# Chunk products with the two heads in turn, and the first block's mixer in another order

## The chip, the core and the metric

The kernel runs on one core of a Trainium2 chip. The metric is the device time of one execution in microseconds (us), the median of three runs. A core has TensorE (PE, with its weight loads listed apart as PEld), VectorE (DVE), ScalarE (ACT), GpSimd (POOL) and SyncE (SP), each with an instruction queue of its own that runs in order. Three of them issue DMAs here: SP, ACT and POOL.

## The reference, cut to what matters

Two transformer blocks of depth 2 each run one after the other on 512 tokens with 1024 channels. The change touches the attention and convolution part ("mixer") of the first block and the gated delta net of the second.

```python
# first block, per layer, between two feed-forward nets
q, k, v, ca, cg = jnp.split(u @ w_in[i], SPLITS, axis=-1)      # 512, 128, 128, 512, 512 columns
q = _partial_rope(q.reshape(B, S, 8, 64), positions)           # 8 heads of 64
k = _partial_rope(k.reshape(B, S, 2, 64), positions)           # 2 key heads
attn = _sliding_window_attention(q, k, v, sinks[i])            # blocks of 128, window 128, softmax with a sink
conv = _conformer_conv(ca, cg, conv_w[i], ...)                 # ca*sigmoid(cg), 31 taps per channel, layer norm, silu
mixed = jnp.concatenate([_rms_norm(attn, ...), _rms_norm(conv, ...)], axis=-1)
h = h + mixed @ w_out[i]

# second block, per layer: gated delta rule in chunks of 64 tokens, 6 heads of 64
lower = jnp.where(strict, einsum('bhncd,bhnsd->bhncs', k_beta, k) * decay, 0.0)   # per head, chunk: 64x64
sol = triangular_solve(lower, concatenate([v * beta, k_beta * exp(g)]), lower=True, unit_diagonal=True)
attn = einsum('bhncd,bhnsd->bhncs', q, k) * decay
# then a scan over the 8 chunks with a 64x64 state per head
```

## The kernel before, in words

Activations stand transposed: 128 channels on the partitions, 512 tokens along the free dimension. A product with a large weight is done in three matmuls of 512 columns per 128x128 weight tile (`mm3`, lines 258 to 262: high by high, high by low, low by high). The weights come as raw chunks of four tiles (256 KB) through SP's queue, four ahead (`_fetch`); ACT makes the high part (line 233) and VectorE the low part (line 234). Their order in DRAM is the order of use and is fixed on the host (`perm` and `lead`, lines 1734 to 1769).

The order on each engine is made by the framework when the kernel is built: of the instructions whose inputs are ready by its own reckoning, the one that stands earliest in the program goes first. So a unit of filler work that stands in the program between two dependent steps covers the wait between them. Such fillers are Python generators in `self.side`; `fill` takes a number of units from one, and `pace` (line 740) does so at a rate beside a chosen instruction, at most four such instructions ahead (`LAG`).

First block, `mixer1` (line 453). Line 455 starts four columns at once (gate and value of convolution channels 0 and 1); the loop of line 470 computes the eight `ca`/`cg` columns, gates them (lines 473 to 476) and sends each result to DRAM and back (lines 479 and 483, SP's queue), which spreads 32 channels over four shifted copies, `u4` (two buffers). Then come k, v (lines 488 and 489) and four q columns (line 509) with their rotation (`rope`) on VectorE. The convolution `conv(j)` (line 516) builds diagonal weights (line 519) and runs 8 groups of 4 matmuls with 32 output columns each, two instructions per matmul; a group is one filler unit. Attention is `scores(n)`, `values(n)` and `outs(n)` for four blocks of 128 tokens: two score matmuls per head (lines 548 and 549), eviction with mask and minimum (line 552), Exp (line 560), transposes (line 582), copy (line 584) and value products (line 586, through `mm2`, line 267). Convolution groups are paced beside them, 0.6 units per pair of heads in `scores` and 0.8 in `values`, one before the first score, and what is left after the last block (line 621). A layer norm over the four convolution results follows (lines 622 to 641); the products `pA` with the attention half of `w_out` run beside it and those with the other half, `pB`, after it.

Second block, class `Gdn`. Two heads share a tile, one on partitions 0 to 63 and one on 64 to 127. A product per chunk and head is a 64x64 matmul from a head's half of one tile and of another into its half of one PSUM bank; `chunks8` (line 1374) issues all 16 of them. It is called by `swap` (line 1466, a transpose), in `pre` (line 1549), by `mms` (line 1556, six times in each `inverse`) and at the end of `inverse` (line 1634). The scan (line 1648 and on) and `quarters` (line 1616) issue the two heads in turn. Fillers beside all this are the columns of the second block's input product.

PSUM has eight banks. Around the first block they are two `ps`, two `pa`, two `po`, one `px` and one `pc` (line 1689).

Of the kernel before, what the change touches and what calls it, by code (L numbers as in the profile page):

```python
# [13 lines left out]
AF = mybir.ActivationFunctionType  # L14
OP = mybir.AluOpType
# [3 lines left out]
T = 512  # L19
# [20 lines left out]
NSA_SCAN = 1.5  # L40
ORDER = ((0, 0), (1, 0), (0, 1), (1, 1), (2, 0), (2, 1), (3, 0), (3, 1))
DL_ACT = 3
FILL_FIRST = 1
AT_NORM = (4, 5, 4, 3, 3)
SQ_MIX = 1
PE_AT = 4
# [5 lines left out]
SUB_RATE = 0.35  # L52
ROWS = 1
SQ_DVE = 7
FILL_ATT = (.6, .8)
UBUFS = 2
LAG = 4
NEG = -1e30
# [59 lines left out]
class Net:  # L118
# [333 lines left out]

    def mixer1(self, i):
        nc = self.nc
        xs, rs = self.lead("pag", 4, gain=self.vec(f"mix{i}", 0, 8), at=AT_NORM[1])
        con = self.tp.tile([128, 4], F32, name="con", tag="con")
        nc.vector.tensor_scalar(con, self.vec(f"con{i}", 0, 4), 0.5, None, OP.mult)
        nsink = self.tp.tile([128, 8], F32, name="nsink", tag="nsink")
# [8 lines left out]
            nc.vector.tensor_tensor(diag, diag, self.ident[:, a:a + 32], OP.add)  # L467
        self.band = self.tp.tile([128, 256], F32, name="band", tag="band")
        nc.scalar.dma_start(self.band, self.A["band"])
        for j in range(4):  # L470
            pa, pg = self.lin("pag", xs), self.lin("pag", xs)
            a, g = self.t(name="ca", tag="c"), self.t(name="cg", tag="c")
            nc.vector.tensor_tensor(g, pg, rs, OP.mult)
            nc.scalar.activation(g, g, AF.Tanh, scale=0.5)
            nc.vector.tensor_tensor(a, pa, rs, OP.mult)
            nc.vector.scalar_tensor_tensor(a, g, 1.0, a, OP.add, OP.mult)

            um = self.tc.dram_tile([128, T], F32, name="um")
            nc.sync.dma_start(um, a)
            x = self.tp.tile([128, 4, T], F32, name="u4", tag="u4", bufs=UBUFS)  # L480
            nc.gpsimd.memset(x[:, :, 0:3], 0.0)
            for t in range(4):
                nc.sync.dma_start(x[t * 32:t * 32 + 32, :, t:], um.rearrange("(g f) x -> f g x", g=4)[:, :, :T - t])
            U4.append(x)
        cosr, sinr = self.t(name="cosr", tag="q"), self.t(name="sinr", tag="q")
        nc.vector.tensor_tensor(cosr, self.trig[0], rs, OP.mult)
        nc.vector.tensor_tensor(sinr, self.trig[1], rs, OP.mult)
        kr = self.rope(self.lin("pk", xs), cosr, sinr, 8, "qt")
        pv = self.lin("pv", xs)
        vT = self.t(name="vT")  # L490
        nc.vector.tensor_tensor(vT, pv, rs, OP.mult)
        pt = self.pat("vt")
# [13 lines left out]
            ks.append(y)  # L506
            kl.append(low)
        for j in range(4):
            x = self.rope(self.lin("pq", xs), cosr, sinr, 8, "qt")
            for g in range(2):  # L510
                y = self.t(F32R, "qs", "q")
                nc.scalar.copy(y[H[g]], x[H[g]])
                nc.vector.tensor_tensor(y[H[1 - g]], x[H[g]], y[H[g]].bitcast(F32), OP.subtract)
                qs.append(y)

        def conv(j):

            w = self.tp.tile([128, 32, 32], F32, name="cd", tag="cd", bufs=2)
            nc.vector.tensor_tensor(w, diag.unsqueeze(1).to_broadcast([128, 32, 32]),
                                    cs[:, j * 32:j * 32 + 32].unsqueeze(2).to_broadcast([128, 32, 32]), OP.mult)  # L520
            us4, pc = U4[j], self.bank("pc", "pc")
            for q in range(8):
                for g in range(4):
                    nc.tensor.matmul(pc[g * 32:g * 32 + 32, 4 * q:], w[:, g * 8 + q], us4[:, g, :T - 4 * q],
                                     start=q == 0, stop=q == 7, skip_group_check=True)
                yield
            y = self.t(name="y", tag="cp")
            nc.scalar.activation(y, pc, AF.Identity, bias=self.vec(f"cb{i}", j))
            ys.append(y)

        self.side, self.paced = dict(conv=chain(*(conv(j) for j in range(4)))), []
        mixA = [(self.x("mH"), self.x("mL")) for _ in range(4)]
        sink = self.vec(f"sink{i}", 0, 8)
        st = {}
# [1 line left out]
        def scores(n):  # L536
            k0 = max(n - 1, 0)
            w = (n - k0 + 1) * 128
            S = [self.t(name="S", tag="S") for _ in range(4)]
            nm = self.s(8, name="nm")  # L540
            for g in range(2):
                for j in range(4):
                    if j % 2 == 0:
                        ps = self.bank("scores", "sc")
                    hd = g * 4 + j
                    f = slice(j % 2 * 256, j % 2 * 256 + w)
                    q, b, k = qs[2 * j + g], slice(n * 128, (n + 1) * 128), slice(k0 * 128, (n + 1) * 128)
                    nc.tensor.matmul(ps[:, f], q[:, b], ks[g][:, k], start=True, stop=False)
                    last = nc.tensor.matmul(ps[:, f], q[:, b], kl[g][:, k], start=False, stop=True)
                    if j % 2:  # L550
                        self.pace(last, conv=FILL_ATT[0])
                    nc.vector.tensor_tensor_reduce(S[j][:, g * 256:g * 256 + w], ps[:, f],
                                                   self.band[:, 256 - w:], -0.125, nsink[:, hd:hd + 1],
                                                   OP.add, OP.min, nm[:, hd:hd + 1])
            den = self.s(8, name="den")
            for j in range(4):
                for g in range(2):
                    hd = g * 4 + j
                    x = S[j][:, g * 256:g * 256 + w]
                    nc.scalar.activation(x, x, AF.Exp, scale=-1.0, bias=nm[:, hd:hd + 1], accum_out=den[:, hd:hd + 1])  # L560
            es = self.s(8, name="es")
            nc.vector.tensor_tensor(es, sink, nm, OP.add)
            nc.scalar.activation(es, es, AF.Exp)
            nc.vector.tensor_tensor(den, den, es, OP.add)
            rd = self.s(8, name="rd")
            nc.vector.reciprocal(rd, den)
            st[n] = (S, rd)

        def values(n):
            S, rd = st[n]  # L570
            k0 = max(n - 1, 0)
            nk = n - k0 + 1
            w = nk * 128
            po = self.out_ps()
            for hd in range(8):
                j, g = hd % 4, hd // 4
                if hd % 2 == 0:
                    pp = self.pat("pp")
                    pT = self.t(name="pT", tag="p")
                b = (hd % 2) * 256  # L580
                for kb in range(nk):
                    nc.tensor.transpose(pp[:, b + kb * 128:b + kb * 128 + 128],
                                        S[j][:, g * 256 + kb * 128:g * 256 + kb * 128 + 128], self.ident)
                nc.scalar.copy(pT[:, b:b + w], pp[:, b:b + w])
                for kb in range(nk):
                    last = self.mm2(po[:, hd * 64:hd * 64 + 64], pT[:, b + kb * 128:b + kb * 128 + 128],
                                    v[:, (k0 + kb) * 128 + g * 64:(k0 + kb) * 128 + g * 64 + 64],
                                    start=kb == 0, stop=kb == nk - 1)
                if hd % 2:
                    self.pace(last, conv=FILL_ATT[1])  # L590
            st[n] = (po, rd)

        def outs(n):
# [15 lines left out]
            for j in range(4):  # L609
                self.split_to(mixA[j][0][:, c], mixA[j][1][:, c], pt[:, j * 128:(j + 1) * 128], self.vec(f"aon{i}", j))  # L610

        self.fill("conv", FILL_FIRST)
        scores(0)
        for n in range(4):
            if n < 3:
                scores(n + 1)
            values(n)
            if n:
                outs(n - 1)
        outs(3)  # L620
        self.fill("conv", None)
        a, b = self.t(name="ya", tag="c"), self.t(name="yb", tag="c")
        nc.vector.tensor_tensor(a, ys[0], ys[1], OP.add)
        nc.vector.tensor_tensor(b, ys[2], ys[3], OP.add)
# [27 lines left out]
    def ple(self, pT, gain, norm, last=False):  # L652
# [9 lines left out]

        def proj():
            for m in range(8):
                pe = self.out_ps("pe")
                self.linear(pe, ps_)
                e = self.t(name="e", tag="a")
                nc.scalar.copy(e, pe)
                es.append(e)
            r.append(self.rstd_end(self.squares(es, SQ_PE), D))  # L670
# [702 lines left out]

def chunks8(f):

    for _, s in H2:
        for c in range(8):
            f(s, slice(c * 64, c * 64 + 64))


# [291 lines left out]
def build(tc, A, plan, out):  # L1672
    with ExitStack() as ctx:
# [5 lines left out]
        with n.phase(n=2, na=1, r=3), n.psum(ps=2, pa=2, pat=("pa",)):  # L1679
# [3 lines left out]
            for big, steps in groupby(enumerate(plan), lambda x: x[1][:-1] == "mix2_"):  # L1683
                if big:
# [1 line left out]
                        with n.phase(cd=4, gq=5, gs=6, gp=12, gat=3, v=4), tc.tile_pool(name="sp2", bufs=1) as n.sp2:  # L1686
                            n.mixer2(int(step[-1]), at and plan[at - 1] == "fin1_0")
                    continue
                with n.psum(po=2, px=1, pc=1, lin=("ps", "po", "ps", "po", "px"), scores=("ps", "px", "ps"),
                            gate=("ps", "px", "ps", "pc", "po", "po")):  # L1690
                    for at, step in steps:
                        k, i = step[:-1], int(step[-1])
                        after = plan[at + 1] if at + 1 < len(plan) else ""
# [56 lines left out]
def host(I):  # L1750
# [13 lines left out]
    for nm in ("ffn1", "ffn2"):  # L1764
        A[nm] = np.stack([ffn(I[nm + "_w_gate_up"][i], I[nm + "_w_down"][i]) for i in range(2)])
    q = np.concatenate([np.r_[j * 64:j * 64 + 64, (4 + j) * 64:(4 + j) * 64 + 64] for j in range(4)])
    perm = np.concatenate([np.r_[768 + j * 128:896 + j * 128, 1280 + j * 128:1408 + j * 128] for j in range(4)]
                          + [np.r_[512:768], q])
    A["w_in"] = each(I["w_in"], lambda w: pack(w[:, perm], lead([(m, k) for m in range(14) for k in range(8)], 4)))
    A["w_out"] = each(I["w_out"], lambda w: pack(w, [(m, k) for q in ((0, 1, 2, 3), (4, 5, 6, 7)) for m in range(8) for k in q]))  # L1770

# [150 lines left out]
```

## Time and profile before

| | us |
|---|---|
| median of 3 runs | 3725.37 (3722.95 to 3727.85) |
| the profiled execution | 3727.08 |
| its span, first to last instruction | 3725.3 |
| busy in the span: TensorE | 3654.2 |
| VectorE | 2307.7 |
| ScalarE | 1563.1 |
| GpSimd | 155.9 |

The profile is of one execution. Busy time of an engine is the time in which at least one of its instructions is listed as running; the matmuls overlap in their pipeline and their ends are modelled, so a busy TensorE can still be one that runs below its rate. To see that, one looks at when matmuls start. The time of a group of equal matmuls runs from the first one's start to the last one's end. The granted clock is TensorE's clock as a share of 2.4 GHz; the two levels are 1.2 and 2.4 GHz.

### The profile page before, as it was taken

Reading aid. Unit: us, or ns where it says so; the run is one execution under the profiler, and the core shown is the slowest. Engines: PE = TensorE matmul, PEld = TensorE weight load, DVE = VectorE, ACT = ScalarE, POOL = GpSimd, SP = SyncE. Lnnn points to the kernel's source line nnn. Section 1 sums busy time; section 2 is a strip of 40 time slices with the busy share of each in tenths; the row PEclk is TensorE's granted clock in tenths of the full one; section 3 lists DMA queues with packets and bytes.
Section 4 is the critical chain, followed back from the end, with each engine's and each line's share of the span. In section 5 each row is a group of like instructions: output and inputs, shape, how many; then the busy total and the mean of one; then the engine's idle time right before and its main releaser. Section 6 shows DMA issues by size and latency. Waiting matters only on the chain. (4 is left out here: it accounts for less than half of the span.)

```text
span 3725.3 us, 55291 instructions
## 1 busy us (share of the span) xinstructions
PE 3654.2 (98%) x20946; PEld 2902.1 (78%) x20946; DVE 2307.7 (62%) x4820; ACT 1563.1 (42%) x2974; POOL 155.9 (4%) x164
## 2 busy tenths in 40 slices
PE   9999999999999999999999999999999999999998
PEld 7888757888888886688887777778887777778887
DVE  5444666444653456753448777775667786786667
ACT  4233354333532334532335344553445344653345
POOL 0000000000100000100001000000001000000001
PEclk9999999999999999999999999999999999999999
DMA  4333413333333333233333212133334112133332
GB/s 130 97 97 98 118 43 88 98 98 97 99 97 97 98 108 91 56 99 96 97 104 95 66 41 78 48 99 97 97 97 134 49 44 62 54 94 99 97 97 90
DMA packets 178955, 329.84 MB, mean 89 GB/s; under 512 B 20096, under 2 KB 24576, under 8 KB 178688
## 3 DMA queue, kind: packets, MB, share of 16 engines
q1 hardware_dynamic: 171648, 312.00, 29.8%
q10 hardware_dynamic: 5760, 10.12, 0.8%
q0 software_dynamic: 1280, 4.20, 0.3%
q8 instruction: 164, 2.69, 0.3%
q14 instruction: 103, 0.84, 0.1%
HBM read 317.84 MB, written 8.39 MB: 88 GB/s over the span
## 5 line engine op out<-in xcount | busy, mean ns | idle before, releaser
L233 ACT CAST wH<-raw 128x512 fp32r<-128x512 f32 x1116 | 691.7, 621 | 1433.5 <-PE pgu L261 457.6
L234 DVE TENSOR_TENSOR wL<-raw,wH 128x512 fp32r<-128x512 f32 x1116 | 790.7, 709 | 594.6 <-ACT wH L233 564.8
L260 PE MATMUL pgu<-xH,wH 128*128 128x512 f32 x1408 | 549.0, 390 | 9.8 <-ACT wH L233 5.9
L261 PE MATMUL pgu<-xL,wH 128*128 128x512 f32 x1408 | 550.8, 391 | 6.1 <-DVE xL L314 6.1
L262 PE MATMUL pgu<-xH,wL 128*128 128x512 f32 x1408 | 550.4, 391 | 0.8 <-DVE wL L234 0.6
L260 PE MATMUL pd<-H,wH 128*128 128x512 f32 x1056 | 410.8, 389 | 0.0
L261 PE MATMUL pd<-L,wH 128*128 128x512 f32 x1056 | 410.8, 389 | 0.0
L262 PE MATMUL pd<-H,wL 128*128 128x512 f32 x1056 | 410.8, 389 | 0.0
L260 PEld LDWEIGHTS pgu<-xH,wH 128*128 128x128 f32 x1408 | 265.1, 188 | 65.5 <-ACT wH L233 5.9
L261 PEld LDWEIGHTS pgu<-xL,wH 128*128 128x128 f32 x1408 | 265.9, 189 | 61.8 <-DVE xL L314 6.7
L262 PEld LDWEIGHTS pgu<-xH,wL 128*128 128x128 f32 x1408 | 265.9, 189 | 56.9 <-DVE wL L234 1.8
L260 PE MATMUL pup<-xH,wH 128*128 128x512 f32 x704 | 274.8, 390 | 2.1 <-DVE h L899 1.2
L262 PE MATMUL pup<-xH,wL 128*128 128x512 f32 x704 | 274.0, 389 | 0.0
L261 PE MATMUL pup<-xL,wH 128*128 128x512 f32 x704 | 273.9, 389 | 0.0
L260 PEld LDWEIGHTS pd<-H,wH 128*128 128x128 f32 x1056 | 198.2, 188 | 41.3
L261 PEld LDWEIGHTS pd<-L,wH 128*128 128x128 f32 x1056 | 198.2, 188 | 41.1
L262 PEld LDWEIGHTS pd<-H,wL 128*128 128x128 f32 x1056 | 198.2, 188 | 41.0
L349 POOL TENSOR_TENSOR ssum<-ssum,sq 128x512 f32<-128x512 f32 x72 | 110.7, 1537 | 2546.2 <-ACT sq L348 2544.9
L260 PEld LDWEIGHTS pup<-xH,wH 128*128 128x128 f32 x704 | 132.1, 188 | 31.3 <-DVE h L899 2.0
L261 PEld LDWEIGHTS pup<-xL,wH 128*128 128x128 f32 x704 | 132.2, 188 | 27.4
L262 PEld LDWEIGHTS pup<-xH,wL 128*128 128x128 f32 x704 | 132.2, 188 | 27.3
L1350 DVE SCALAR_TENSOR_TENSOR y<-x,vecs,y 128x511 f32<-128x511 f32 (+1 forms) x176 | 131.2, 749 | 17.4 <-ACT y L1347 14.7
(571 smaller groups left out, 6063.1 us busy)
## 6 DMA issues: line engine op xcount, KB each, us to landing
raw<-ffn SPq DMA_DIRECT2D x791, 256.0 KB, 2.6
raw<-w_in SPq DMA_DIRECT2D x164, 256.0 KB, 2.6
raw<-w_out SPq DMA_DIRECT2D x80, 256.0 KB, 2.7
raw<-w_ple_gate SPq DMA_DIRECT2D x80, 256.0 KB, 2.7
away<-h ACTq DMA_DIRECT2D x16, 256.0 KB, 2.1
raw<-cmp SPq DMA_DIRECT2D x16, 256.0 KB, 2.7
h<-away POOLq DMA_DIRECT2D x16, 256.0 KB, 4.2
h<-xT SPq DMA_DIRECT2D x8, 256.0 KB, 5.3
```

The lines of the kernel that those rows point to most:

```text
L233: nc.scalar.copy(H, r)
L234: nc.vector.tensor_tensor(L, r, H.bitcast(F32), OP.subtract)
L260: nc.tensor.matmul(ps, w[0], x[0], start=first, stop=False)
L261: nc.tensor.matmul(ps, w[0], x[1], start=False, stop=False)
L262: nc.tensor.matmul(ps, w[1], x[0], start=False, stop=last)
L349: (nc.vector if k >= adds else nc.gpsimd).tensor_tensor(acc, acc, q, OP.add)
L1350: nc.vector.scalar_tensor_tensor(y[:, s:], x[:, :T - s], w[:, f * 3 + tap:f * 3 + tap + 1], y[:, s:], OP.mult, OP.add)
```

## The change

`chunks8` goes over the chunks and, in each, over the two heads. In `mixer1` k, v and the q columns come first (four of these six in the leading group). The `ca`/`cg` columns become a generator `gated(j)` with one unit per triple of matmuls, gate column first; its DRAM round trip goes through POOL's queue. A convolution is one unit in place of eight. Columns and convolutions form one chain of fillers, 16 units of it ahead of the first scores, then 1.8 per pair of heads in `scores` and 2 in `values`; what is left comes before the last `outs`. The banks are dealt anew: scores rotate over the two `ps`, attention values use one `po`, the new columns use `px` and a new `py`. On the host the columns of `w_in` are permuted to match.

```diff
-FILL_FIRST = 1
+FILL_FIRST = 16
-FILL_ATT = (.6, .8)
+FILL_ATT = (1.8, 2)
@@ mixer1
-        xs, rs = self.lead("pag", 4, gain=self.vec(f"mix{i}", 0, 8), at=AT_NORM[1])
+        xs, rs = self.lead("pkvq", 4, gain=self.vec(f"mix{i}", 0, 8), at=AT_NORM[1])
...
-        for j in range(4):
-            pa, pg = self.lin("pag", xs), self.lin("pag", xs)
-            a, g = self.t(name="ca", tag="c"), self.t(name="cg", tag="c")
-            nc.vector.tensor_tensor(g, pg, rs, OP.mult)
-            nc.scalar.activation(g, g, AF.Tanh, scale=0.5)
-            nc.vector.tensor_tensor(a, pa, rs, OP.mult)
+
+        def gated(j):
+
+            g, a = self.t(name="cg", tag="c"), self.t(name="ca", tag="c")
+            for x, name in ((g, "pg"), (a, "pa")):
+                p = self.bank("cols", name)
+                yield from self.linear_g(p, xs)
+                nc.vector.tensor_tensor(x, p, rs, OP.mult)
+                if x is g:
+                    nc.scalar.activation(g, g, AF.Tanh, scale=0.5)
             nc.vector.scalar_tensor_tensor(a, g, 1.0, a, OP.add, OP.mult)
 
             um = self.tc.dram_tile([128, T], F32, name="um")
-            nc.sync.dma_start(um, a)
+            nc.gpsimd.dma_start(um, a)
             x = self.tp.tile([128, 4, T], F32, name="u4", tag="u4", bufs=UBUFS)
             nc.gpsimd.memset(x[:, :, 0:3], 0.0)
             for t in range(4):
-                nc.sync.dma_start(x[t * 32:t * 32 + 32, :, t:], um.rearrange("(g f) x -> f g x", g=4)[:, :, :T - t])
+                nc.gpsimd.dma_start(x[t * 32:t * 32 + 32, :, t:], um.rearrange("(g f) x -> f g x", g=4)[:, :, :T - t])
             U4.append(x)
...
@@ conv(j)
                 for g in range(4):
                     nc.tensor.matmul(pc[g * 32:g * 32 + 32, 4 * q:], w[:, g * 8 + q], us4[:, g, :T - 4 * q],
                                      start=q == 0, stop=q == 7, skip_group_check=True)
-                yield
             y = self.t(name="y", tag="cp")
             nc.scalar.activation(y, pc, AF.Identity, bias=self.vec(f"cb{i}", j))
             ys.append(y)
-
-        self.side, self.paced = dict(conv=chain(*(conv(j) for j in range(4)))), []
+            yield
+
+        self.side, self.paced = dict(fill=chain(gated(0), gated(1), conv(0), gated(2), conv(1), gated(3), conv(2), conv(3))), []
...
@@ end of attention
-        self.fill("conv", FILL_FIRST)
+        self.fill("fill", FILL_FIRST)
         scores(0)
...
+        self.fill("fill", None)
         outs(3)
-        self.fill("conv", None)
@@ ple
-                pe = self.out_ps("pe")
+                pe = self.bank("pe", "pe")
@@ chunks8
-    for _, s in H2:
-        for c in range(8):
+    for c in range(8):
+        for _, s in H2:
             f(s, slice(c * 64, c * 64 + 64))
@@ build
-                with n.psum(po=2, px=1, pc=1, lin=("ps", "po", "ps", "po", "px"), scores=("ps", "px", "ps"),
-                            gate=("ps", "px", "ps", "pc", "po", "po")):
+                with n.psum(po=1, px=1, py=1, pc=1, lin=("ps", "po", "ps", "py", "px"), scores=("ps",), cols=("px", "py"),
+                            gate=("ps", "px", "ps", "pc", "po", "py"), pe=("po", "py")):
@@ host
-    perm = np.concatenate([np.r_[768 + j * 128:896 + j * 128, 1280 + j * 128:1408 + j * 128] for j in range(4)]
-                          + [np.r_[512:768], q])
+    perm = np.concatenate([np.r_[512:768], q] + [np.r_[1280 + j * 128:1408 + j * 128, 768 + j * 128:896 + j * 128] for j in range(4)])
```

## Rows read from the trace of the kernel before

**Rows 1.** The page, section 1: busy us, share of the span, instructions

```profile
PE 3654.2 (98%) x20946; PEld 2902.1 (78%) x20946; DVE 2307.7 (62%) x4820; ACT 1563.1 (42%) x2974; POOL 155.9 (4%) x164
```

**Rows 2.** Timeline of PE, one chunk product: start, length, line, count

```profile
2065.58 1.90 PE L1549 MATMUL pkk<-kb,y 64*64 64x64 f32 x32
2067.40 0.50 PE L261 MATMUL pqkv<-xL,wH 128*128 128x512 f32 x1
```

**Rows 3.** Timeline of PE, two chunk products back to back and their seam

```profile
2118.27 1.72 PE L1556 MATMUL py<-X,TT 64*64 64x64 f32 x29
...
2119.94 0.22 PE L1556 MATMUL pyt<-TT,X 64*64 64x64 f32 x1
2119.95 0.22 PE L1556 MATMUL py<-X,TT 64*64 64x64 f32 x1
2120.00 1.67 PE L1556 MATMUL pyt<-TT,X 64*64 64x64 f32 x29
2121.60 0.50 PE L260 MATMUL psq<-xH,wH 128*128 128x512 f32 x1
```

**Rows 4.** Timeline of PE, a step of the scan

```profile
2143.61 0.33 PE L1648 MATMUL pvd<-S,kbg 64*64 64x64 f32 x4
```

**Rows 5.** Windows: length, busy of PE, PEld, DVE, ACT, POOL; granted clock; DMA

```profile
452.60:459.00 6.40, 3.17 (x19) 2.42 (x17) 6.22 (x21) 5.51 (x16) 0.00 (x0) 0.94 0.23 59
459.00:470.00 11.00, 10.99 (x56) 4.14 (x55) 4.49 (x22) 4.72 (x22) 0.00 (x0) 0.72 0.04 14
...
452.60:528.50 75.90, 72.64 (x594) 32.06 (x592) 38.92 (x158) 38.37 (x129) 0.23 (x2) 0.96 0.16 36
...
1444.00:1463.00 19.00, 17.01 (x82) 8.15 (x84) 10.12 (x39) 10.05 (x35) 0.00 (x0) 0.73 0.11 28
```

**Rows 6.** Timeline of PE, a score of block 0; in brackets the wait

```profile
455.25 0.33 PE L548 MATMUL sc<-ks,qs 128*128 128x128 f32 x1 [1.80 <-DVE nm L552]
```

**Rows 7.** Convolution matmuls: group over attention (busy, mean ns), then timeline of two pieces

```profile
L524 PE MATMUL pc<-u,cd 128*32 128x500 f32 (+7 forms) x232 | 41.9, 611 | 0.0
...
494.14 1.02 PE L524 MATMUL pc<-u,cd 128*32 128x488 f32 x6
...
521.02 5.25 PE L524 MATMUL pc<-u,cd 128*32 128x512 f32 x48
```

**Rows 8.** Windows of lines 1466 and 1634: length, PE and PEld busy, counts

```profile
2020.00:3300.00 1280.00, 37.99 (x576) 34.72 (x576) 0.99 0.26 75
...
2020.00:3300.00 1280.00, 21.52 (x384) 20.20 (x384) 0.99 0.26 75
```

**Rows 9.** Windows, 80 us of the second block's first mixer

```profile
2040.00:2120.00 80.00, 71.16 (x582) 57.00 (x581) 66.07 (x185) 24.06 (x41) 3.11 (x4) 0.91 0.25 77
```

**Rows 10.** Timeline of PE at the first products after the layer norm

```profile
553.28 0.39 PE L262 MATMUL pB<-xH,wL 128*128 128x512 f32 x1
...
553.96 0.39 PE L262 MATMUL pB<-xH,wL 128*128 128x512 f32 x1
554.90 0.73 PE L260 MATMUL pB<-xH,wH 128*128 128x512 f32 x2 [0.56 <-ACT xH L313]
```

**Rows 11.** Timeline of PE in the second block's sparse attention

```profile
2392.50 0.69 PE L267 MATMUL pos<-nv,pT 128*64 128x64 f32 x16
2393.12 0.50 PE L1283 MATMUL pss<-kws,q0s 128*128 128x512 f32 x1
```

**Rows 12.** DMA issues: queue, count, KB, us to landing; then a line's min/median/max ns

```profile
um<-ca SPq DMA_DIRECT2D x8, 256.0 KB, 3.0
u<-um SPq DMA_DIRECT2D x8, 255.0 KB, 5.9
h<-away POOLq DMA_DIRECT2D x16, 256.0 KB, 4.2
L875 POOL DMA_DIRECT2D h<-away x16: 536/537/707, 2267.6 to 3122.8; - x16
```

**Rows 13.** Instructions of line 560: min/median/max ns, first and last start

```profile
L560 ACT ACT_TABLE_LOAD  x2: 1283/1283/1283, 453.3 to 1444.8; - x2
```

More of the change, by code (lines that the diff above doesn't have):

```diff
@@ L487, in mixer1 @@
         nc.vector.tensor_tensor(sinr, self.trig[1], rs, OP.mult)
-        kr = self.rope(self.lin("pk", xs), cosr, sinr, 8, "qt")
-        pv = self.lin("pv", xs)
+        kr = self.rope(self.lin("pkvq", xs), cosr, sinr, 8, "qt")
+        pv = self.lin("pkvq", xs)
         vT = self.t(name="vT")
@@ L508, in mixer1 @@
         for j in range(4):
-            x = self.rope(self.lin("pq", xs), cosr, sinr, 8, "qt")
+            x = self.rope(self.lin("pkvq", xs), cosr, sinr, 8, "qt")
             for g in range(2):
@@ L550, in scores @@
                     if j % 2:
-                        self.pace(last, conv=FILL_ATT[0])
+                        self.pace(last, fill=FILL_ATT[0])
                     nc.vector.tensor_tensor_reduce(S[j][:, g * 256:g * 256 + w], ps[:, f],
@@ L589, in values @@
                 if hd % 2:
-                    self.pace(last, conv=FILL_ATT[1])
+                    self.pace(last, fill=FILL_ATT[1])
             st[n] = (po, rd)
```

## The prediction

> **What bounds the kernel now.** I read the page's first section, then the stage windows of the two stretches that the change edits, then the order of instructions on TensorE in them. TensorE is busy for 98% of the span [rows 1], so time is won only where TensorE's own work gets shorter or where it waits. The change touches two places.
>
> The first is the chunk products of the second block's gated delta net. One `chunks8` call is 16 products of 64x64, each two matmul instructions: first all eight chunks of one head (partitions 0 to 63), then all eight of the other (64 to 127). One call's 32 instructions take 1.90 us and the next matmul starts 1.82 us after the first [rows 2]. Less 0.22 us for the last one, that is 1.68 / 31 = 0.054 us per instruction. At the seam between two calls the picture differs: the last matmuls of one (second head) and the first of the next (first head) start in pairs, 0.01 us apart, and the pairs follow every 0.06 us [rows 3]. So two heads can run side by side, each at its full rate. Where the code already alternates (the scan's pair of heads), four instructions take 0.33 us [rows 4], of which the last one alone is 0.22.
>
> The second place is the attention of the first block. It lasts 75.9 us in layer 0, with PE listed as busy for 72.64 [rows 5], but not at its rate. In the first 6.4 us PE is busy for 3.17; one score waited 1.80 us for the score eviction on VectorE [rows 6]. The granted clock is 0.72 over the next 11 us and 0.73 over the first 19 of layer 1 [rows 5], so part of that time is at the lower level, 1.2 GHz, right after PE had sat waiting. The convolution matmuls take 41.9 us for 232 instructions, while an unbroken row of 48 takes 5.25 us; a torn-off group of six takes 1.02 us, 0.17 each against 0.11 [rows 7].
>
> **Part 1, alternating heads.** The two lines with 576 instructions and the two with 384 (the first and the last of the four stand in [rows 8]) make 1920, which is 60 calls of 32. New cost of a lone call: 0.11 us to the second pair (0.33 - 0.22 in [rows 4]), 14 more pairs at 0.058 and 0.15 until the next matmul (1.82 - 1.68): 1.07 us instead of 1.82, so 0.75 saved. Two calls back to back take 2118.27 to 2121.60 = 3.33 us now [rows 3]; new 0.11 + 30 x 0.058 + 0.15 = 2.0, so 0.66 saved per call. I count 20 calls in such pairs (pattern of [rows 3]): 40 x 0.75 + 20 x 0.66 = 43 us. Not all of it arrives. In the 80 us in which the first layer's mixer gets going, VectorE is busy for 66.07 and PE already stands idle for 8.8 [rows 9]; there VectorE's chain is late next. The second layer is alike. About 19 of the 60 calls lie in these two stretches; I count them at half, 19 x 0.37 = 7. Elsewhere PE is full and dense products fill every wait. **Part 1: -36 us**, bounds -27 (those 19 at nothing, and 2 us lost to VectorE elsewhere) and -44 (all).
>
> **Part 2, the mixer's new order.** The columns of k, v and q now come first; 64 triples of column matmuls (0.68 us each, 553.28 to 553.96 in [rows 10]) and four convolutions become 68 filler units, 16 ahead of the first scores, then 1.8 or 2 per pair of heads. The matmul work is the same.
> (a) Start of attention. Idle and clock lost in layer 0: (6.40 - 3.17) + 0.28 x 11.0 = 6.3 us; layer 1: (19.0 - 17.0) + 0.27 x 19 = 7.1 [rows 5]. Now 16 triples, 10.9 us, stand ahead of the first score, and 1.2 us of columns follow each pair of heads where 0.6 of a conv group (0.5 us) did. That covers rope and evictions: -11 us for both layers (bounds 0 to -14).
> (b) Whole convolutions. 232 instructions at 5.25/48 each would be 25.4 us; 41.9 - 25.4 = 16.5 lost per layer, 3.1 of it the clock of (a). A convolution is now one unit, but attention instructions that stand earlier in the program still break into it as they become ready, so I take 5 of the 13 per layer: -10 us (bounds 0 to -26).
> (c) Columns wedged between heads. In the second block's sparse attention, which is filled that way, 16 value products take 0.69 - 0.22 = 0.47 us from first to last start, and the next matmul, of another shape, starts 0.62 after the first [rows 11]: a changeover of 0.15 us. Here 68 units meet 32 heads, where conv groups paid the same before. I add ten more changeovers, +1.5 us a layer (bounds 0 and 32 x 0.15 = 4.8): +3.
> (d) The last convolution. Each column's result goes to DRAM and back in five transfers, now on POOL's queue in place of SP's. SP's transfers took 3.0 and 5.9 us to land; the only POOL ones in this trace took 4.2, with POOL busy 0.54 us for each [rows 12]. Round trip: two VectorE steps 1.4, write 4.2, four issues 2.1, last landing 5.9: 13.6 us (bounds 10 with SP's landings, 20 under contention). The first three convolutions have 16 column triples (10.9 us) plus the heads between them, some 25 us, as cover. The fourth has only the third convolution (some 7 us) and the last block's values and outputs (about 10). If it is late, the layer norm behind it is late for the `pB` products, which wait 0.56 us already [rows 10]. I take 0 for it (bounds -2 to +10 a layer).
> Costed at nothing: the 20 issues per layer that leave SP (weight fetches queue there, and no matmul waits for a raw weight in the rows I read) and their 10.8 us on POOL, busy 0.23 us in this stretch [rows 5]; the queued work behind POOL's wait for a free `u4` buffer is only the next column's transfers. Two score banks in place of three and one `po` bank in place of two: the first value product of a block waits for the 0.7 us read of the block before; fillers cover it, +3 us a layer if not. Tanh between Exp: the Exp table is loaded once per layer [rows 13], and the Tanh of line 638 after it brought no further load.
> **Part 2: -11 - 10 + 3 + 0 = -18 us**, bounds about -44 and +24.
>
> **Sum.** -36 - 18 = -54 us. The profiled execution took 3727.1 us (span 3725.3 and 1.8 around it), which gives 3673; the median of the three runs is 1.7 lower, so I forecast 3671.
>
> **Rivals.**
> - *Only part 1 arrives*: conv pieces stay torn, the fourth convolution is late, (a) pays for it. 3725 - 36 + 0 to 12 = 3689 to 3701. For it: the end of the chain is already tight [rows 10]. Against: (a) is plain idle time.
> - *More arrives*: convolutions run nearly whole and VectorE is no brake: 3725 - 43 - 37 = 3645.
> - *The heads do not overlap inside a call*, since both halves write the same PSUM bank: then part 1 is 0 and the time 3725 - 18 = 3707. Against it: the scan's four products in [rows 4] write two halves of one bank and take 0.33 us, where one after the other they would need 0.11 + 2 x 0.058 + 0.22 = 0.45. The Trainium skill's page "TensorEngine Tiling (Array Packing)", section "Restrictions and Gotchas", states this rule: different row tiles cannot access the same PSUM bank simultaneously. By it the change would gain only part 2; the scan's row speaks against it here.
> - *Slower*: the round trip through POOL is longer than its cover, and PE's queue, which runs in order, stands behind each convolution's first matmul. Four convolutions a layer lose (trip - 25) each; with 54 us to eat up, it decides from 25 + 54/8 = 32 us on, and a trip of 40 us gives 3671 + 8 x 15 = 3791. Against it: 13.6 us by the rows, and nothing over 10 us to landing.
> - *Nothing changes* in the end (VectorE takes back what PE saves): 3725.
>
> **How the numbers follow.** Forecast 0.60 (3652 to 3688), only part 1 0.17, more 0.10, no overlap 0.07, slower 0.04, nothing 0.02. The range takes in the second and third: 3640 to 3703. This kernel's measurement can tell about 0.2% (7.5 us) from no change, so all cases but the last two count as faster: 0.94, same 0.02, slower 0.04.
>
> **What would show it.** Right: a `chunks8` call of 32 rows in about 1.15 us instead of 1.90, with PE's busy time down by about 50 us; no score waiting over 1 us at the start of attention and a granted clock near 1.0 there; the convolution matmuls well under 41.9 us a layer. Wrong: calls still at 1.90 us; conv matmuls held by a POOL transfer; `pB` starting with a wait of several us; PE idle growing in the first 80 us of each second-block mixer, by as much as the calls shrink.

## The result

The changed kernel takes 3668.95 us (median of four runs, 3664.8 to 3675.47) against 3725.65 for the kernel before on the same chip: ratio 0.985, 95% interval 0.9832 to 0.9868. The forecast was 3671. The sum came out about 2 us off, but not all its terms did: several were mis-sized, in opposite directions.

The profiled execution took 3664.8 us (span 3663.0), the fastest of the four; the profiled one of before, 3727.08, was among the slower of its own. So the two profiles lie 62 us apart and the medians 57. Stage lengths, read from the starts of the first matmul of each stage in the two timelines (us):

| stage | before | after |
|---|---|---|
| first block's mixers, first column to the next feed-forward matmul, both layers | 412.5 | 393.6 |
| of it first column to first `pA`, layer 0 and layer 1 | 157.0, 155.3 | 147.2, 146.3 |
| second block's mixers, both layers | 876.9 | 833.1 |
| all the rest of the span | 2435.9 | 2436.3 |

So between these two executions 18.9 us come from part 2's place and 43.8 from part 1's, and nothing moved elsewhere. About 5 of the 18.9 hang on the clock in this one execution of the kernel before, as the run with heads alone shows below. The page's first section (busy us, share, instructions), which answers [rows 1], agrees: TensorE is busy 64.6 us less with the same instructions, VectorE and ScalarE the same.

```profile
PE 3589.6 (98%) x20946; PEld 2852.8 (78%) x20946; DVE 2306.2 (63%) x4820; ACT 1563.1 (43%) x2974; POOL 176.8 (5%) x204
```

**A chunk product.** Timeline of PE (start, length, line, count); the first two rows answer [rows 2], the others [rows 3]. This seam lies in line 1640, between the two products of one step:

```profile
2102.48 1.15 PE L1472 MATMUL psw<-ident,y 64*64 64x64 f32 x32
2103.56 0.69 PE L1622 MATMUL pyt<-TT,X 32*32 32x32 f32 x32
...
2106.91 1.08 PE L1640 MATMUL puw<-vb,TT 64*64 64x64 f32 x29
2107.79 0.22 PE L1640 MATMUL puw<-TT,kbg 64*64 64x64 f32 x1
2107.84 0.22 PE L1640 MATMUL puw<-vb,TT 64*64 64x64 f32 x1
2107.84 1.14 PE L1640 MATMUL puw<-TT,kbg 64*64 64x64 f32 x31
```

The next matmul starts 1.08 us after the first, where [rows 2] had 1.82. At the seam the two calls still mingle, by two instructions now.

**The first 80 us of the second block's mixer**, windows (length; busy and count of PE, PEld, DVE, ACT, POOL; granted clock; DMA share, GB/s), which answer [rows 9]:

```profile
2021.30:2091.90 70.60, 62.01 (x581) 47.85 (x580) 63.70 (x183) 24.15 (x41) 3.11 (x4) 0.95 0.28 87
2026.00:2106.00 80.00, 72.47 (x736) 56.02 (x736) 71.96 (x203) 26.68 (x44) 3.11 (x4) 0.96 0.24 74
```

Counted in matmuls from the mixer's first, the first line is the stretch of [rows 9]; the second has its length, from 5 us later in the program on. The same matmuls take 70.6 us in place of 80, and PE's idle time stays about the same, 8.6 us against 8.8. In 80 us 736 matmuls run instead of 582, and VectorE rises from 66.07 to 71.96. The four longest waits listed are the same in both, 4.1, 3.3, 0.6 and 0.5 us; VectorE added none.

**The start of attention**, the same view, which answers [rows 5]:

```profile
403.60:410.00 6.40, 4.71 (x20) 3.18 (x19) 6.30 (x12) 2.12 (x4) 0.00 (x0) 1.00 0.16 41
403.60:423.00 19.40, 17.54 (x78) 13.30 (x77) 18.36 (x37) 10.49 (x21) 0.69 (x1) 1.00 0.32 95
...
1378.00:1397.00 19.00, 17.23 (x76) 13.40 (x75) 18.67 (x34) 9.72 (x17) 0.00 (x0) 1.00 0.19 56
```

The granted clock is 1.00 where it was 0.72 and 0.73. PE waits a little, but for something else. PE's waits over layer 0's whole mixer (total, times, longest) were three of 2.7 us in all for `nm` and one of 0.5 for `qs`, longest 1.80 [rows 6]; now they are:

```profile
PE po L267 <- ACT pT L589: 2.0, 5, 0.5
PE pkvq L262 <- DVE wL L234: 0.9, 1, 0.9
PE pg L262 <- DVE wL L234: 0.8, 1, 0.8
PE pA L260 <- ACT mH L313: 0.5, 1, 0.5
PE sc L553 <- DVE nm L557: 0.2, 1, 0.2
```

VectorE, busy for 6.30 of the first 6.40 us, makes low parts of weights, and two column matmuls wait for them.

**Convolutions.** The group of both layers (busy, mean ns), which answers [rows 7], whose group covers layer 0's attention alone. Before:

```profile
L524 PE MATMUL pc<-u,cd 128*32 128x500 f32 (+7 forms) x512 | 88.3, 616 | 0.0
```

After:

```profile
L529 PE MATMUL pc<-u,cd 128*32 128x492 f32 (+7 forms) x512 | 59.7, 583 | 0.0
```

28.6 us less, some 3 of it the clock: the run with heads alone, with the convolutions as before, has 85.3. The end of layer 0's attention shows the rest, and what is left; timeline of PE, in brackets the wait:

```profile
494.10 1.06 PE L529 MATMUL pc<-u,cd 128*32 128x512 f32 x8
495.09 0.45 PE L267 MATMUL po<-v,pT 128*64 128x64 f32 x8
495.47 6.02 PE L529 MATMUL pc<-u,cd 128*32 128x508 f32 x54
501.43 0.65 PE L612 MATMUL ot<-ident,o 128*128 128x128 f32 x4
...
502.82 0.45 PE L267 MATMUL po<-v,pT 128*64 128x64 f32 x8 [0.52 <-ACT pT L589]
...
510.58 6.89 PE L529 MATMUL pc<-u,cd 128*32 128x512 f32 x64
517.40 0.66 PE L612 MATMUL ot<-ident,o 128*128 128x128 f32 x4
518.53 0.73 PE L260 MATMUL pA<-mH,wH 128*128 128x512 f32 x2 [0.48 <-ACT mH L313]
```

A convolution is torn once or twice, by a head's value product, and then runs 54 to all 64 matmuls in a row. From 501.4 to 510.6 the last block's values run bare, with five waits of 0.18 to 0.52 us for ScalarE's copy: the third convolution is used up and the fourth stands behind them. Its columns' trip, timeline of POOL and then DMA issues (count, KB, us to landing), which answer [rows 12]:

```profile
493.92 0.56 POOL L483 DMA_DIRECT2D um<-ca  x1 [21.40 <-DVE ca L480]
497.35 2.19 POOL L487 DMA_DIRECT2D u<-um  x4 [2.87 <-DMA um<-ca]
```

```profile
um<-ca POOLq DMA_DIRECT2D x8, 256.0 KB, 2.9
...
u<-um POOLq DMA_DIRECT2D x8, 254.5 KB, 5.5
```

From the first issue to the last landing that is about 497.35 + 4 x 0.55 - 0.55 + 5.5 - 493.92 = 10.6 us. So the data were there at 504.5, the diagonal weights at 473.1, and ScalarE had read the third convolution out of the one `pc` bank by 502.2. The fourth starts only at 510.58, without a wait: for 6 us nothing on the chip held it but its place in PE's order, which was fixed when the kernel was built. The products behind the layer norm, which waited 0.56 us before [rows 10], now start without a wait:

```profile
543.06 0.39 PE L260 MATMUL pB<-xH,wH 128*128 128x512 f32 x1
543.29 0.39 PE L261 MATMUL pB<-xL,wH 128*128 128x512 f32 x1
```

### The profile page after: what moved, and what is told of

Read it like the earlier page. It is cut to its first block, busy times and chain, and to the rows that moved or that the text cites. A ratio compares the mean times of both kernels' runs of the same rounds, so it can differ in the third digit from the quotient of the medians.

```text
span 3663.0 us, 55287 instructions
## 1 busy us (share of the span) xinstructions
PE 3589.6 (98%) x20946; PEld 2852.8 (78%) x20946; DVE 2306.2 (63%) x4820; ACT 1563.1 (43%) x2974; POOL 176.8 (5%) x204
## 5 line engine op out<-in xcount | busy, mean ns | idle before, releaser
L260 PE MATMUL pgu<-xH,wH 128*128 128x512 f32 x1408 | 550.0, 391 | 10.3 <-ACT wH L233 6.3
```

Source lines behind the costliest of these rows:

```text
L260: nc.tensor.matmul(ps, w[0], x[0], start=first, stop=False)
```

## The experiments

"First mixers" below are the first block's two layers as in the table's first row, "second mixers" its third. Four kernels each ran on one chip, with its own runs of the kernel before: 3722.63 us for heads alone, the mixer alone, groups and the third buffer, 3722.13 for four chunks, SP's queue, the first later fillers and coarse columns, and 3721.67 for the last four.

**Each part alone.** Heads in turn, and nothing else:

```diff
-    for _, s in H2:
-        for c in range(8):
+    for c in range(8):
+        for _, s in H2:
```

> The kernel before with the heads of chunks8 in turn and nothing else. Theory (the two parts add up, and PE's saved time arrives in full): each of the 60 calls takes 1.08 us to the next matmul in place of 1.82, the two second-block mixers shrink by some 43 us together, time 3725.7 - 43 = 3683. Rival (VectorE takes some of it back in the first 80 us of each mixer, as the prediction had it): -36, 3690.

Measured 3683.13 us (3682.32 to 3683.76), ratio 0.9892, interval 0.9879 to 0.9906: 39.5 us, midway between the two cases. The stages decide: the second mixers take 834.4, as in the full change, 42.5 less than before.

This run is also a control for part 2, since its first mixers are those of the kernel before. They take 407.6 us, not 412.5. In layer 1 a score waits the same 1.80 us, but the clock stays up; windows, as the last line of [rows 5]:

```profile
1444.00:1463.00 19.00, 16.86 (x103) 8.43 (x101) 12.46 (x46) 12.21 (x43) 0.10 (x1) 1.00 0.15 37
```

That layer's mixer takes 200.8 us in place of 205.2, 2.8 of it in the convolution's line and 1.5 in the scores'. So the loss of clock there belongs to one execution of the kernel before, and against 407.6 the full change wins 14.0 in the first mixers, not 18.9.

The full change without that edit:

> The changed kernel with chunks8 as before: the first block's new order alone. Theory: the first block's two mixers shrink by 19 us together, the second block stays as it was, time 3707. Rival (the two parts touch each other, through the order of instructions or the clock): not within 5 us of that.

Measured 3710.28 (3704.84 to 3715.24), ratio 0.9964, interval 0.995 to 0.9978: 12.4 us. The first mixers take 395.7, 16.8 less than in the profile of before and 11.9 less than in the run with heads alone, which fits the 12.4; the second ones 881.8, 5 more, with short stretches at 1.2 GHz that the first profile of before does not have there. The parts add up: 39.5 + 12.4 = 52, and both together gave 57 in the first comparison and 47 in the last (below).

**How far two heads overlap.** Four chunks of one head, then four of the other:

```diff
-    for c in range(8):
-        for _, s in H2:
-            f(s, slice(c * 64, c * 64 + 64))
+    for o in range(0, 8, 4):
+        for _, s in H2:
+            for c in range(o, o + 4):
+                f(s, slice(c * 64, c * 64 + 64))
```

> The changed kernel with chunks8 taking four chunks of one head, then the same four of the other. Theory (PE starts a matmul of the other head once at most three older matmuls of the first are unstarted, as the seams of the kernel before show): of 32 instructions the first four and the last four run alone and the other 24 in twelve pairs, so twenty starts of 0.058 us, 1.31 us to the next matmul against 1.08 in the changed kernel, 60 x 0.23 = 14 us in all, time 3683. Rival (PE looks far enough ahead that the order inside a call matters little): 1.08 us, 3669. Second rival (only direct neighbours overlap): 1.7 us, 3706.

Measured 3689.07 (3687.51 to 3692.37). Timeline of PE:

```profile
2107.81 1.54 PE L1473 MATMUL psw<-ident,y 64*64 64x64 f32 x32
2109.27 0.69 PE L1623 MATMUL pyt<-TT,X 32*32 32x32 f32 x32
```

The call takes 1.46 us, between one head after the other (1.82) and heads in turn (1.08), and more than my theory gave. The second mixers take 856.0, 22.9 more than in the changed kernel, which is 60 calls of 0.38. The starts of the 32 instructions of one such call say where it erred. The first head's come at 0, 0.11, 0.17, 0.22, 0.28 us, and the second head's first at 0.29, right behind the fifth of eight: three older ones had not started, as the theory said. But in each group of eight the second instruction comes 0.11 us after the first and only the later ones follow at 0.058; that step comes four times here and once with heads in turn. So a matmul on the other half of the array can start ahead of three older ones, and the order of issue decides how much overlaps.

**Whole convolutions or groups.** The changed kernel with eight units per convolution again and a rate to match:

```diff
-FILL_ATT = (1.8, 2)
+FILL_ATT = (2.5, 2.8)
...
                     nc.tensor.matmul(pc[g * 32:g * 32 + 32, 4 * q:], w[:, g * 8 + q], us4[:, g, :T - 4 * q],
                                      start=q == 0, stop=q == 7, skip_group_check=True)
+                yield
             y = self.t(name="y", tag="cp")
...
-            yield
```

> The changed kernel with each convolution in eight units again, at 2.5 and 2.8 units per pair of heads so that the fillers last as long. Theory (whole convolutions are worth what the trace shows, 12 us a layer less in the convolution matmuls): the pieces come back, 58 us for the 512 convolution matmuls become some 80, time 3669 + 18 = 3687. Rival (what broke them up was attention without other filler): 3669 within 4.

Measured 3677.69 (3676.37 to 3679.08), first mixers 407.4, 13.8 more than the changed kernel. The group of convolution matmuls accounts for 13.1 of it:

```profile
L529 PE MATMUL pc<-u,cd 128*32 128x484 f32 (+7 forms) x512 | 72.8, 587 | 0.0
```

That lies between the theory and the rival. So the larger unit, with its rate, is worth 13 of the 28.6 us that this line lost; the other 15 came with the order, in which convolutions run at the full clock and with fewer pieces even as groups.

**The queue of the round trip.** Both `dma_start` of `gated` back on SP:

```diff
-            nc.gpsimd.dma_start(um, a)
+            nc.sync.dma_start(um, a)
...
-                nc.gpsimd.dma_start(x[t * 32:t * 32 + 32, :, t:], um.rearrange("(g f) x -> f g x", g=4)[:, :, :T - t])
+                nc.sync.dma_start(x[t * 32:t * 32 + 32, :, t:], um.rearrange("(g f) x -> f g x", g=4)[:, :, :T - t])
```

> The changed kernel with the columns' DRAM round trip on SP's queue, where it was before. Theory (the queue is neither a brake nor a gain; POOL's trip of some 10.6 us from write to last landing is covered): 3669 within 4. Rival (on SP a write that waits for its column holds the weight fetches queued behind it, so PE waits for weights): the first block's mixers grow by 5 us or more each, 3679 or more.

Measured 3671.53 (3664.85 to 3673.3), first mixers 393.0 against 393.6. The queue neither costs nor gains.

**The hole before the fourth convolution.** A third `u4` buffer, with the fourth columns ahead of the second convolution in the chain:

```diff
-UBUFS = 2
+UBUFS = 3
...
-        self.side, self.paced = dict(fill=chain(gated(0), gated(1), conv(0), gated(2), conv(1), gated(3), conv(2), conv(3))), []
+        self.side, self.paced = dict(fill=chain(gated(0), gated(1), conv(0), gated(2), gated(3), conv(1), conv(2), conv(3))), []
...
-                            with n.phase(q=15, qt=2, S=8, t=2, p=2, o=3, c=8, cp=4):
+                            with n.phase(q=15, qt=2, S=8, t=2, p=2, o=3, c=6, cp=4):
```

> The changed kernel with three u4 buffers (two of the column tiles' eight given up for it) and the last columns before the second convolution, so that the last convolution's input is there early. Theory: in the changed kernel the values of the last block run bare, with four waits of up to 0.5 us, since the last convolution stands behind them; now convolutions fill them: 3 us a layer, time 3669 - 6 = 3663. Rival: columns then run out earlier and the hole only moves: 3669.

Measured 3666.83 (3665.92 to 3670.83), first mixers 395.6. The hole moved: with its columns there early, the fourth convolution was drawn early too, and the last outputs stood bare. Timeline of PE:

```profile
514.66 0.66 PE L612 MATMUL ot<-ident,o 128*128 128x128 f32 x4
519.87 1.08 PE L612 MATMUL ot<-ident,o 128*128 128x128 f32 x4 [4.54 <-DVE o L609]
```

The granted clock fell to 0.50 for 6.8 us from 519.0 on, 3.7 us into that wait. What was missing is filler at the end. So the next kernel keeps three buffers and draws fillers later:

```diff
-FILL_ATT = (1.8, 2)
+FILL_ATT = (1.5, 1.8)
```

> The kernel with the third u4 buffer, at 1.5 and 1.8 units per pair of heads. Theory (with 1.8 and 2 all convolutions are used up before the last outputs, which then wait 4.8 us bare): at the slower rates three convolutions are left for the last block's values and outputs, no wait over 1 us is left there, 5 us a layer less than with the faster rates: the first block's mixers come to 388 us in sum, time 3660. Rival (the later convolutions hold up the layer norm, and the products behind it wait): 3669 or more.

Measured 3663.04 (3657.79 to 3665.34), first mixers 386.1.

The opposite size, columns in units of two triples with half the rate:

```diff
-FILL_FIRST = 16
+FILL_FIRST = 8
...
-FILL_ATT = (1.8, 2)
+FILL_ATT = (.9, 1)
...
-                yield from self.linear_g(p, xs)
+                for k, _ in enumerate(self.linear_g(p, xs)):
+                    if k % 2:
+                        yield
```

> The changed kernel with two triples of column matmuls to a unit, at half the rates. Theory (every unit wedged between heads costs changeovers: column matmuls lose 7 us a layer in the changed kernel against 1 in the kernel before): half of that comes back, 3 us a layer, time 3663. Rival (larger units come too rarely, and scores and values wait instead): 3669 or more.

Measured 3674.05 (3672.38 to 3675.37), first mixers 401.5. Its loss is the same hole: a convolution is one unit still, at half the rate, so the chain runs later and the fourth convolution comes after the outputs' wait:

```profile
507.64 0.45 PE L267 MATMUL po<-v,pT 128*64 128x64 f32 x8 [0.46 <-ACT pT L591]
512.71 1.09 PE L614 MATMUL ot<-ident,o 128*128 128x128 f32 x4 [4.61 <-DVE o L611]
513.72 6.63 PE L531 MATMUL pc<-u,cd 128*32 128x512 f32 x48
```

The theory fails apart from that: the columns of layer 0 take 83.8 us from start to start in place of 84.0, and 94 of their matmuls still stand beside another shape, against 101 in the changed kernel. Larger units did not bring clearly fewer changeovers, so what fewer would be worth stays open.

**Rate and buffer, taken apart**, four kernels on one chip. The third buffer always comes with the fourth columns ahead of the second convolution, so these two stay together. The changed kernel itself:

> The changed kernel itself, beside the next three on one chip, so that a few us between them can be told. Expected 3669 (3665 to 3675), and two layers of the first block's mixer at about 393 us together, as in its first profile.

Measured 3675.12 (3673.2 to 3677.42), ratio 0.9866, interval 0.9849 to 0.9884; first mixers 395.6, second 843.9 (833.1 in the first profile; the last section has most of the reason). Its rate alone changed, to (1.6, 1.8):

> The changed kernel with the later fillers alone (1.6 and 1.8 units per anchor in place of 1.8 and 2), and its two column buffers. Theory: the hole in the changed kernel is that the fourth convolution must wait for columns whose round trip (10.6 us) starts only when a buffer is free, so that the last block's values run bare; later fillers alone move the second and third convolutions later too, which covers about half of the hole: 3665, first mixer 389. Rival, the rate alone does it and the third buffer is not needed: 3662, first mixer 386, as with three buffers. Other rival, the fourth convolution comes later by as much and nothing is won: 3669.

Measured 3688.24 (3677.64 to 3691.09), first mixers 405.9: none of the three expected cases, but 13 us slower than the changed kernel. Timeline of POOL, then of PE:

```profile
497.03 0.56 POOL L483 DMA_DIRECT2D um<-ca  x1 [23.41 <-DVE rs L326]
500.21 2.18 POOL L487 DMA_DIRECT2D u<-um  x4 [2.62 <-DMA um<-ca]
```

```profile
507.14 0.45 PE L267 MATMUL po<-v,pT 128*64 128x64 f32 x8 [0.46 <-ACT pT L589]
512.21 1.09 PE L612 MATMUL ot<-ident,o 128*128 128x128 f32 x4 [4.62 <-DVE o L609]
...
517.03 6.89 PE L529 MATMUL pc<-u,cd 128*32 128x512 f32 x64
```

The trip starts 3.1 us later than in the changed kernel and the fourth convolution 6.5 later, behind the outputs and into the `pA` products. The outputs' chain on VectorE then has no cover, 4.6 us, and the clock is 0.50 for 6.8 us from 510.2 on, 2.6 us into that wait. The two layers lose 10 us. The trip itself had ended by then: its last landing is at 507.6 (501.84 + 5.8), just when the wait begins. So the fourth convolution could have filled the wait and stood behind it in PE's order. That the framework reckoned with a later landing when it made that order is likely, but not shown.

With the third buffer:

> Three column buffers and later fillers (1.5 and 1.8), run again beside the changed kernel: 3662 to 3665 and first mixer 386 by the theory that the fillers' place was the loss; 3669 if the earlier reading was the luck of a run.

Measured 3662.07 (3658.09 to 3664.25), ratio 0.9832, interval 0.9816 to 0.9848; first mixers 386.3. And with (1.35, 1.6):

> Three buffers and still later fillers (1.35 and 1.6). Theory: 1.5 and 1.8 already spread the units to the end of attention, so that still later ones are drawn after it in a row, while the last block's outputs have no more cover needed: within 2 us of the run with 1.5 and 1.8, about 3664, first mixer 387. Rival, early attention still has units to give: 3660. Other rival, the score waits at the start of attention come back, with fewer units between, and the clock with them: 3671.

Measured 3658.86 (3656.63 to 3659.36), ratio 0.9823, interval 0.9809 to 0.9838; first mixers 384.4, 1.9 under the rates before, nearer to the first rival than to the theory. This beats both kernels: 62.8 us under the kernel before, 16.3 under the changed one on the same chip. Of the 16.3, 11.2 stand in the first mixers; the rest is in the second ones, which the edit does not touch. Timeline of PE:

```profile
492.95 5.17 PE L529 MATMUL pc<-u,cd 128*32 128x504 f32 x46
498.06 0.66 PE L612 MATMUL ot<-ident,o 128*128 128x128 f32 x4
498.92 6.89 PE L529 MATMUL pc<-u,cd 128*32 128x512 f32 x64 [0.21 <-ACT y L532]
505.74 0.50 PE L260 MATMUL pA<-mH,wH 128*128 128x512 f32 x1
```

The second convolution covers the last values, the third the outputs' chain, and the fourth runs among the `pA` products. In this stretch nothing runs bare and no wait is over 0.21 us.

## Why the prediction was right, point by point

**Part 1, mechanism and size.** A lone call was put at 1.07 us and takes 1.08. With 60 calls, 20 of them in pairs, the full sum was 43 us; the stages gave 43.8, and part 1 alone 42.5 in the stages (876.9 to 834.4) and 39.5 in the medians. The step that failed is the discount of 7 us for the first 80 us of each mixer. I had read a VectorE busy for 66 of 80 us as the engine that is late next. The same matmuls took 9.3 us less there and 7.5 less in the second layer's stretch: 16.8, where 19 calls in full are 14 and I had counted 7. VectorE still had 7 of the 70.6 us left, and PE's waits stayed the same. A high busy share alone does not say that an engine would hold the path.

The rival that heads do not overlap because both halves write one PSUM bank is out: the call would have stayed at 1.82 us. The Trainium skill's page "TensorEngine Tiling (Array Packing)", section "Restrictions and Gotchas", states that different row tiles cannot access one PSUM bank at the same time, and would have given that time. For 64x64 tiles that write two partition halves of one bank, the trace does not agree, 1.08 against 1.82. The scan's row [rows 4], which spoke against it, was the better guide.

**Part 2, right sum of wrong terms.** To size them in layer 0, I took the time from each matmul's start to the next one's and summed it by line, from the first column to the first `pB`. The matmuls are the same before and after. In all it was 181.3 us before and 171.7 after, 9.6 less where 9 a layer was predicted.

- *(a) Start of attention*: as predicted in kind. The long score waits and the half clock are gone, and the scores' lines lost 5.9 us in layer 0 (15.1 to 9.2) where 5.5 was taken. The clock is the weak part of this term: the 5.1 us put down to it in layer 1 measured 4.4, and another execution of the same code did not lose them.
- *(b) Whole convolutions*: a mis-sized term. I took 5 of 13 us a layer, for fear that attention's instructions would tear the units. The line lost 12.8 in layer 0 (42.3 to 29.5; 27.5 in unbroken rows), at most 3.1 of it the clock that is counted in (a): nearly all that was to be had. A unit is torn only where a head's value product becomes ready, once or twice in a convolution.
- *(c) Columns wedged between heads*: the other mis-sized term. I took 1.5 us a layer with a bound of 4.8; the columns cost 7.1 more (76.9 to 84.0). Two waits for low parts of weights are 1.7 of it. The rest lies at the column matmuls that stand beside another shape: 101 of them lost 5.5 us where three had lost 0.2 in the same stretch before. I had counted ten more changeovers of 0.15 us for the heads; but a triple is itself split, and single column matmuls stand between pairs of scores and of transposes. The value products lost 1.4 more.
- *(d) The last convolution*: 0, as taken, in the products behind the layer norm. From its first issue the trip was 10.6 us where 12.2 was put down (13.6 less 1.4 for VectorE's steps), mostly as POOL's writes landed in 2.9 us, not in the 4.2 of the nearest row. But the fourth convolution's place in PE's order left the bare stretch of 9 us in the last block's values, with 2.0 us of waits in layer 0, which I had not priced. With two buffers and later fillers that place cost 10 us in two layers, though the trip ended in time for the wait there too.

In layer 0, -5.9 - 12.8 + 7.1 + 1.4, with 0.6 of smaller lines, is -9.6. (b) was too small a gain by some 5 to 8 and (c) too small a cost by 5.6 and the value products' 1.4; that they cancel is luck. So is the agreement of 18.9 with the 18 predicted: against the first mixers of the run with heads alone it is 14.0, and part 2 alone gave 12.4 in the medians. Part 1's needless discount made up for that. The upper bound of part 2 was also added up wrongly: 4.8 and 10 a layer make about +30, not +24.

**Costed at nothing, and nothing**: the queue (393.0 on SP against 393.6 on POOL), one `po` bank in place of two (no wait of a value product for its bank is listed), the function table (as many loads as before). The rival "only part 1 arrives" (3689 to 3701) stood 20 to 32 us off, and part 1 alone measured 3683. "Slower", by a round trip of over 32 us, never came near: 10.6 from the first issue.

## What to carry to other kernels

Where two products sit on different halves of the array, issue them in turn: the order inside a run of small matmuls decided 40 us here, at the same instructions. A filler's worth depends on where the last ones stand; look for the last dependent chain (values, outputs, norm), count what is left to cover it, and slow the rate until something is left. Read in the trace when its input landed, and compare that with when it starts: where it starts later without a wait, its place in the order is what has to move; here columns that stood earlier in the program moved it. When two terms of a sum are uncertain, a good total does not confirm either; split the change on the chip, and look at what the unedited stages do in those runs: here one of them moved by 5 us.

## What the runs showed of the hardware

Two 64x64 matmul streams in opposite halves, a product each in turn, run at 0.058 us per pair of instructions, though they write the same PSUM bank, and one can start ahead of three older ones on the other half. So TensorE, unlike what the first section says of every queue, does not start its matmuls strictly in order.

The same instructions in the same order can meet another clock in another execution. In the second block's second mixer of the changed kernel PE waits 0.58 and 0.59 us for VectorE (`hs`) in the two executions profiled; 2 us later one of them fell to 1.2 GHz for 17.1 us and the other did not. Windows of the one that fell:

```profile
3087.00:3104.00 17.00, 17.00 (x97) 11.64 (x96) 8.66 (x29) 4.77 (x17) 0.00 (x0) 0.50 0.06 17
```

and of the other, at the same place in the program:

```profile
3082.50:3099.50 17.00, 16.88 (x168) 11.91 (x168) 12.65 (x46) 9.23 (x29) 0.53 (x1) 1.00 0.07 18
```

97 matmuls against 168 in 17 us; that mixer took 422.9 us against 414.7, with 6.8 of the 8.2 lost here (the same 96 matmuls took 17.1 and 10.3 us). The two executions, of one and the same kernel, took 3677.4 and 3664.8 us, and this is why the runs above are compared by their stages too. The start of attention in layer 1 of the kernel before is the other such place, with 4.4 us. What decides it between two such executions stays open: no run here varied it alone.
